# A hybrid diffusion layer: the inverse of the second recurrence multiplied head by head, outputs stored in two pieces a half step, operands loaded by halves of the heads

## The chip, the core and the metric

The kernel runs on one core of a Trainium2 chip. The metric is the device time of one execution in microseconds (us), lower is better. A core has five engines with queues of their own: TensorE (PE) multiplies matrices into PSUM, VectorE (DVE), ScalarE (ACT) and GpSimd (POOL) work element by element, and SyncE (SP) issues the transfers between memory (HBM) and the on-chip SBUF, which 16 DMA engines carry out. Each engine works through its instructions in the order in which the program has them, and waits where one needs a result that isn't there.

## The reference

One layer on 1024 latent tokens and 256 context tokens, 1024 channels wide, all in fp32. A normalised and modulated input goes through one projection into two token mixers: a gated linear recurrence (RG-LRU) and RWKV-7. Their outputs are gated, projected, merged and added to the input; a SwiGLU channel mixer and a last normalisation follow. The change lies in RWKV-7's recurrence, which has 16 heads of 64 channels and runs over the tokens in both directions (`d` = 2), with the context's final state as the start of the latent scan:

```python
def step(S, inp):
    r_t, w_t, k_t, v_t, a_t, b_t = inp
    sa = jnp.einsum('dbhij,dbhj->dbhi', S, a_t)
    S = S * w_t[..., None, :] + sa[..., :, None] * b_t[..., None, :] + v_t[..., :, None] * k_t[..., None, :]
    y = jnp.einsum('dbhij,dbhj->dbhi', S, r_t)
    return S, y
```

The outputs of both directions are added, normalised per head (group norm), joined by a bonus term and multiplied by a gate.

## The kernel before

The program has stages. `phase_ux` and `phase_a2` compute the projections and prepare RWKV-7's operands; `phase_b` runs its recurrence, with the output projection of the RG-LRU as fill; `phase_c1` and `phase_c2` do the merge, the output projection and the channel mixer.

The recurrence works in chunks of 32 tokens: 40 steps, of which steps 0 to 7 are the context and 8 to 39 the latent tokens. Each step handles one chunk in either direction for 16 heads, 32 units of a direction and a head. They are cut into two halves of 8 heads (`a` = 0, 1), and `wkv_chain(k, a)` is a generator that issues one half's work. Inside a chunk the serial dependence is solved by the inverse of a 32 by 32 triangular matrix per unit, made in `phase_a2` by VectorE (`wkv_inverse`, tile `X`), written to HBM as `x_d` and loaded for four steps at a time as `xc`.

One half step is this chain:

- `ru`, first part (line 1034): 16 products of 128 rows by 32 columns, `skb` with `tvu`, into PSUM; a copy brings them to SBUF as `rs` (line 1036).
- `ru`, second part (lines 1045 and 1046): the inverse times `rs`. The four units that stand at partitions 0, 32, 64 and 96 are done by one product of 128 by 128 whose left side is block-diagonal. That left side is the tile `xbd`, cleared once; four VectorE copies a step put the blocks of `xc` into it (line 1025), for both halves, in two tiles that take turns.
- Four copies of 32 partitions bring the result into `tvu` (line 1048), on VectorE and ScalarE in turn (`copy`, line 993).
- `pn` (line 1054): 16 products of 128 rows by 64 columns, the next state; two copies or scalings bring it into the next step's `tvu` (lines 1059 and 1063).
- `py` (line 1005), for latent steps: 16 products, a copy to `ys`, and four stores to `y_d` of 32 rows by 256 numbers (line 1013).

`tvu` has two buffers a half; its rows of v are loaded one step ahead (`new_tvu`, line 969). `wkv_load` (line 982) loads a step's `skb` (1 MB) and `ska` (0.5 MB) into a ring of three, 8 KB a partition in one piece, once both halves are done with the step two before.

In `phase_b` the two halves are drawn in a fixed pattern (line 1158), and between them products of the fill (`pol`, line 1107) in a number that grows with the step. The first eight steps are given a priority over the end of `phase_a2`, which prepares the last heads' operands (`pm`, `pkt`, `pz`) and the last inverses. From step 28 on the group norms of finished token blocks run beside the chain (`norms`, `group_norm`), each loading y of both directions whole (line 1246). A scheduler orders the instructions of each engine by priorities and its own estimate of times, so the order on an engine isn't the order in the code. PSUM tiles that two engines read are read in turn.

Of the kernel before, what the change touches and what calls it, by code (L numbers as in the profile page):

```python
# [16 lines left out]
P = 128  # L17
D = 1024
KD = D // P
SEQ = 1024  # L20
# [887 lines left out]
FILLA = 0  # L908
ROUNDS = ((0, 1), (2, 3), (4, 5), (6, 7), (8,), (9,))
FPTS = ((0, 0), (38, 1), (40, 1))  # L910
UT = 0
NEND = 3
SETV = 0
SETDVE = 0
XDVE = 40
XACT = 0
PACE = 1
MORE = (1, 2, 3)
NRD = 3
# [6 lines left out]
NRING = 3  # L926
# [3 lines left out]
def wkv_setup(k):  # L930
    nc, bp = k.nc, k.bp
    z = lambda n, sh: bp.tile(sh, F32, name=n)
    k.ska = [z(f"ska{i}", [P, NU, 64]) for i in range(NRING)]
    k.skb = [z(f"skb{i}", [P, NU, 64]) for i in range(NRING)]
    for i, t in enumerate(k.ska):
        nc.scalar.copy(t[0:64], bcast(k.ident[0:64, 0:64], 1, NU))
    if not UT:
        k.xbd = [z(f"xbd{i}", [P, 8, 4, 32]) for i in range(2)]
        for t in k.xbd:
            (nc.vector if SETDVE & 2 else nc.gpsimd).memset(t, 0.0)  # L940
    k.tvu = [[z(f"tvu{a}_{i}", [P, 2, 8, 64]) for i in range(2)] for a in range(2)]
    k.pb = z("pb", [P, 2, 20, KD])
    for i, e in ((1, slice(16, 20)), (0, slice(0, 16))):
        for d in range(2):
            nc.sync.dma_start(k.pb[64 * d:64 * d + 64, :, e].rearrange("p h e j -> p h (e j)"),
                              k.pd_d[i][:, d].rearrange("(h p) f -> p h f", p=64))
    k.xc = {}
# [17 lines left out]
def new_tvu(k, s, a):  # L965
    nc = k.nc
    src = pair(k.v_d.rearrange("(c s) f -> c s f", s=32), chunk_id(s, 0), chunk_id(s, 1))
    t = k.tvu[a][s % 2]
    nc.sync.dma_start(t[64:96].rearrange("p d h i -> p d (h i)"), src[:, :, a * 512:a * 512 + 512].rearrange("d s f -> s d f"))
    return t  # L970


def wkv_load(k, s):
    nc = k.nc
    ska, skb = k.ska[s % NRING], k.skb[s % NRING]
    if s % 4 == 0:
        xc = k.bpool.tile([P, 4, 2, 4, 32], F32, name=f"xc{s}", tag="xc", bufs=2)
        nc.sync.dma_start(xc.rearrange("p n a v t -> p (n a v t)"), (k.x_d[:, s - 8:s - 4] if s >= 8 else k.xc_d[:, s:s + 4]).rearrange("p s f -> p (s f)"))
        k.xc[s // 4] = xc
    lat, c = s >= 8, s - 8 if s >= 8 else s  # L980
    for t, src in ((skb, k.skb_d), (ska[64:P], k.ska_d)):
        nc.sync.dma_start(t.rearrange("p u f -> p (u f)"), src[not lat][c].rearrange("r u f -> r (u f)"))


def wkv_chain(k, a):

    nc, pool, ps = k.nc, k.bpool, k.psb

    def mm(*a, **b):
        k.pe_last = nc.tensor.matmul(*a, **b, start=True, stop=True).ins.name  # L990

    def copy(out, src):
        (nc.vector.tensor_copy if k.turn % 5 in COPYD else nc.scalar.copy)(out, src)  # L993
        k.turn += 1

    unit = lambda d, i: d * NH + a * 8 + i
    units = [(v, g, slice(32 * g, 32 * g + 32), g // 2, (g % 2) * 4 + v) for v in range(4) for g in range(4)]

    def outputs(s, tvu):
        if s < 8:  # L1000
            return
        skb = k.skb[s % NRING]
        py = k.psb2.tile([P, 4, 64], F32, name=f"py{s}_{a}", tag="py", bufs=1)
        for v, g, gr, d, i in units:
            mm(py[gr, v], skb[:, unit(d, i), 0:32], tvu[:, d, i])
        ys = k.op.tile([P, 256], F32, name=f"ys{s}_{a}", tag="ys", bufs=4)
        copy(ys, py.rearrange("p v i -> p (v i)"))
        for d in range(2):
            r = 32 * chunk_id(s, d)
            for h in range(2):  # L1010
                g = 2 * d + h
                c = a * 512 + h * 256
                nc.sync.dma_start(k.y_d[d, r:r + 32, c:c + 256], ys[32 * g:32 * g + 32])

    cur, nxt, prev = None, new_tvu(k, 0, a), None
    for t in k.tvu[a]:
        (nc.vector if a < SETV else nc.gpsimd).memset(t[96:P], 0.0)
    for s in range(NSTEP):
        ska, skb = k.ska[s % NRING], k.skb[s % NRING]
        if not UT:  # L1020
            xb = k.xbd[s % 2]
        if a == 0 and not UT:
            for g in range(4):
                gr = slice(32 * g, 32 * g + 32)
                (nc.scalar.copy if s < XACT else nc.vector.tensor_copy if s < XDVE else nc.gpsimd.tensor_copy)(xb[gr, :, g], k.xc[s // 4][gr, s % 4].rearrange("p a v t -> p (a v) t"))
        prev, tvu = cur, nxt
        cur = tvu
        ahead = lambda: new_tvu(k, s + 1, a) if s + 1 < NSTEP else None
        if a == 1:
            nxt = ahead()  # L1030
        t = ps.tile([P, 2, 4, 64], F32, name=f"ru{s}_{a}", tag="ru", bufs=2)
        seen = slice(0 if s else 64, P)
        for v, g, gr, d, i in units:
            mm(t[gr, 0, v], skb[seen, unit(d, i), 32:64], tvu[seen, d, i])
        r = pool.tile([P, 4, 64], F32, name=f"rs{s}_{a}", tag="rs", bufs=2)
        copy(r, t[:, 0])
        yield
        if a == 0:
            if s > 0:
                outputs(s - 1, prev)  # L1040
            nxt = ahead()
            yield
        for v, g, gr, d, i in units if UT else ():
            mm(t[gr, 1, v], k.xc[s // 4][gr, s % 4, a, v], r[gr, v])
        for v in range(0 if UT else 4):
            mm(t[:, 1, v], xb[:, a * 4 + v].rearrange("p a b -> p (a b)"), r[:, v])
        for g in range(4):
            copy(tvu[96:P, g // 2, g % 2 * 4:g % 2 * 4 + 4], t[32 * g:32 * g + 32, 1])
        yield
        if nxt is not None:  # L1050
            pn = (k.psb2 if a and s >= 8 else ps).tile([P, 8, 64], F32, name=f"pn{s}_{a}", tag="pn", bufs=1)
            for i in range(8):
                for d in range(2):
                    mm(pn[64 * d:64 * d + 64, i], ska[0 if s else 64:P, unit(d, i)], tvu[0 if s else 64:P, d, i])
            for d in range(2):
                h = slice(64 * d, 64 * d + 64)
                nt = nxt[0:64, d]
                if s % 2 == 0:
                    copy(nt, pn[h])
                else:  # L1060
                    b1, c1 = chunk(s + 1, d)
                    pv = k.pb[h, :, b1 * 2 + c1 // 2, a * 4:a * 4 + 4].rearrange("p h j -> p j h")
                    nc.vector.tensor_tensor(nt.rearrange("p (j h) i -> p j h i", h=2), pn[h].rearrange("p (j h) i -> p j h i", h=2), bcast(pv, 3, 64), ALU.mult)
        yield
        if a == 1:
            outputs(s, tvu)
            yield
    if a == 0:
        outputs(NSTEP - 1, cur)
        yield  # L1070
# [67 lines left out]
def phase_b(k):  # L1138
    tc = k.tc
    k.gnp = k.root.enter_context(tc.tile_pool(name="gnp", bufs=1, side="right"))  # L1140
    with tc.tile_pool(name="bp", bufs=1) as k.bp, tc.tile_pool(name="olp", bufs=1) as op, \
# [9 lines left out]
        with tc.high_priority(offset=SETO):  # L1151
            wkv_setup(k)
            for s in range(NRING):
                wkv_load(k, s)
        k.turn = 0
        halves = [wkv_chain(k, a) for a in range(2)]
        for s in range(NSTEP + 1):
            for i, a in enumerate((0, 0, 1, 0, 1, 1, 0, 1)):
                if s == 0 and i in (2, 4) or s == NSTEP and i not in (1, 2, 4):
                    continue  # L1160
                if s < CTXP:
                    prio_next(k, halves[a], CTXO)
                else:
                    next(halves[a])
                if i == 4 and s - 1 + NRING < NSTEP:
                    wkv_load(k, s - 1 + NRING)
                if i == 4:
                    k.step = s - 1
                if i == 4 and s == 28:
                    back = norms(k, k.gnp, pso)  # L1170
                if (s, i) >= (28, 4):
                    next(back, None)
                k.pe_after = k.pe_last
                if i in FILLAT:
                    at = s + (FILLAT.index(i) + 1) / len(FILLAT)
                    while done < (480 - FILL0 - TAIL) * (at + CTXW * min(at, 8)) / (NFEND + 8 * CTXW):
                        next(fill, None)
                        done += 1
                k.pe_after = None
# [54 lines left out]
def group_norm(k, pool, ps, tb, out=None):  # L1234
# [7 lines left out]
    flat = lambda t: t.rearrange("p a i -> p (a i)")  # L1242
    y, v, g = big("gy"), big("gv"), big("gg")
    y1 = k.c1p.tile([P, NH, 64], F32, name="gy1_7") if tb == 7 else big("gy1")
    for t, src in ((v, k.v_d), (g, k.gate_d), (y, k.y_d[0]), (y1, k.y_d[1])):
        nc.sync.dma_start(flat(t), src[tok])
        for _ in range(GNY):
            yield
    yield
# [251 lines left out]
def scratch(k):  # L1501
# [13 lines left out]
    k.x_d = t("x_d", [P, NSTEP - 8, 256])  # L1515
    k.pd_d = [t(f"pd{i}_d", [P, 2, n * KD]) for i, n in enumerate((16, 4))]
    k.t1_d = t("t1_d", [D, SEQ])
    k.y_d = t("y_d", [2, SEQ, D])


@with_exitstack
# [174 lines left out]
```

## Time and profile before

| | us |
|---|---|
| median of 3 runs (3169.22 to 3175.68) | 3172.0 |
| the profiled execution | 3170.86 |
| its span | 3168.8 |
| TensorE busy (87%) | 2772.7 |
| VectorE busy (63%) | 2010.8 |
| ScalarE busy (45%) | 1410.4 |
| GpSimd busy (33%) | 1037.3 |

The recurrence begins near 1500 us and ends near 2195. Beside its first 200 us the stage before it ends; in its last 200 us the group norms run. From about 2230 us to the end the span is the merge and the channel mixer, with TensorE nearly without a gap. TensorE's granted clock is a share of 2.4 GHz and has two levels, 1 and 0.5; a mean between them tells how long it was at either. Busy time of TensorE includes the modelled ends of its products, so a stretch in which small products follow each other with pauses of a few hundred ns still counts as busy.

### The profile page before, as it was taken

What the parts mean: (1) busy time and instruction counts of PE and PEld (TensorE: products, weight loads), DVE (VectorE), ACT (ScalarE), POOL (GpSimd) and SP (SyncE); (2) the same over time, 40 slices, a digit from 0 to 9 for tenths busy, and PEclk for the clock granted to TensorE, in tenths of its full rate; (3) what the DMA queues carried; (4) which work ended last, traced back from release to release, by engine and by line L of the source; (5) the groups of instructions that cost most, each with busy time, mean ns of one, the idle gap of its engine ahead of it and who ended that gap; (6) DMA issues with size and microseconds to landing.
All of it is one profiled execution on the core that took longest, in us unless ns stands there. A gap on an engine that the chain in (4) does not pass through costs nothing. (4 is left out here: it accounts for less than half of the span.)

```text
span 3168.8 us, 53672 instructions
## 1 busy us (share of the span) xinstructions
PE 2772.7 (87%) x20606; PEld 2235.2 (71%) x20606; DVE 2010.8 (63%) x3067; ACT 1410.4 (45%) x2579; POOL 1037.3 (33%) x896
## 2 busy tenths in 40 slices
PE   5888888789898878887889878788899999999998
PEld 4767666667777666765666767566678888888888
DVE  7688989894667887878874434675686423232234
ACT  3465757474467555767333433344425111111114
POOL 4344435452445545666333220323441000000000
PEclk9999899999899878987558978788999999999999
DMA  5334333322455455555766777776772211111112
GB/s 201 105 107 128 115 109 118 111 76 74 142 145 143 114 123 128 131 140 136 192 189 213 220 210 206 222 240 220 266 284 85 98 57 54 37 57 40 46 57 71
DMA packets 374726, 428.96 MB, mean 135 GB/s; under 512 B 135446, under 2 KB 279238, under 8 KB 366534
## 3 DMA queue, kind: packets, MB, share of 16 engines
q1 hardware_dynamic: 374470, 425.53, 45.4%
q8 instruction: 163, 2.67, 0.4%
q14 instruction: 93, 0.76, 0.1%
HBM read 286.87 MB, written 126.26 MB: 130 GB/s over the span
## 5 line engine op out<-in xcount | busy, mean ns | idle before, releaser
L88 PE MATMUL pin<-h1024hi,whi 128*128 128x512 f32 (+1 forms) x1024 | 431.9, 422 | 47.0 <-DVE whi L230 15.2
L90 PE MATMUL pin<-h1024hi,wlo 128*128 128x512 f32 (+1 forms) x1024 | 425.8, 420 | 26.0 <-POOL wlo L231 16.8
L89 PE MATMUL pin<-h1024lo,whi 128*128 128x512 f32 (+1 forms) x1024 | 427.2, 417 | 4.1 <-DVE h1024lo L120 4.1
L231 POOL TENSOR_TENSOR wlo<-wraw,whi 128x512 fp32r<-128x512 f32 (+1 forms) x144 | 229.7, 1595 | 339.8 <-DVE whi L230 135.0
L88 PEld LDWEIGHTS pin<-h1024hi,whi 128*128 128x128 f32 (+1 forms) x1024 | 205.2, 201 | 100.8 <-DVE whi L230 21.3
L90 PEld LDWEIGHTS pin<-h1024hi,wlo 128*128 128x128 f32 (+1 forms) x1024 | 204.8, 200 | 80.6 <-POOL wlo L231 23.1
L89 PEld LDWEIGHTS pin<-h1024lo,whi 128*128 128x128 f32 (+1 forms) x1024 | 204.2, 199 | 51.3 <-DVE h1024lo L120 6.6
L54 ACT ACT_TABLE_LOAD x164 | 210.4, 1283 | 17.2 <-DVE gd L499 5.9
L990 PE MATMUL pn<-tvu,ska 128*64 128x64 f32 (+1 forms) x2496 | 159.8, 255 | 34.9 <-DVE tvu L993 20.1
L1444 DVE TENSOR_TENSOR sil<-sil,pfu 128x512 f32<-128x512 f32 x44 | 30.2, 687 | 243.2 <-PE pfu L90 243.2
L990 PEld LDWEIGHTS pn<-tvu,ska 128*64 128x64 f32 (+1 forms) x2496 | 122.8, 161 | 75.9 <-DVE tvu L993 23.3
L388 DVE SCALAR_TENSOR_TENSOR lxc<-lup,c_lru_conv_w,lxc 120x512 f32<-120x512 f32 (+3 forms) x198 | 159.4, 835 | 0.4
L1452 DVE SCALAR_TENSOR_TENSOR x<-pfo,modv,x 128x512 f32<-128x512 f32 (+1 forms) x112 | 74.2, 670 | 132.4 <-PE pfo L90 132.4
L990 PE MATMUL ru<-tvu,skb 128*32 128x64 f32 (+1 forms) x2560 | 107.7, 260 | 49.9 <-ACT tvu L993 26.0
L993 ACT COPY tvu<-ru 32x256 f32<-32x256 f32 x193 | 69.9, 362 | 151.8 <-DVE tvu L993 99.4
L68 ACT CAST whi_fi<-wraw_fi 128x1024 fp32r<-128x1024 f32 x48 | 50.6, 1053 | 168.3 <-PE pfg L89 53.0
L990 PE MATMUL ru<-rs,xbd 128*128 128x64 f32 x640 | 113.3, 335 | 12.4 <-ACT rs L993 8.3
L415 PE MATMUL pg<-lh,gw 120*120 120x512 f32 (+3 forms) x264 | 95.4, 373 | 32.4 <-DVE lh L398 29.7
L990 PEld LDWEIGHTS ru<-tvu,skb 128*32 128x32 f32 (+1 forms) x2560 | 69.5, 131 | 75.9 <-ACT tvu L993 28.5
L680 ACT COPY bc<-pm 32x256 f32<-32x256 f32 x160 | 98.5, 616 | 52.6 <-PE pm L676 50.3
L721 DVE TENSOR_TENSOR X<-X,it 128x62 f32<-128x62 f32 (+25 forms) x186 | 119.1, 640 | 3.9
L720 DVE TENSOR_TENSOR it<-bp,X 128x62 f32<-128x62 f32 (+25 forms) x186 | 118.3, 636 | 3.8
(374 smaller groups left out, 7660.8 us busy)
## 6 DMA issues: line engine op xcount, KB each, us to landing
skb<-skb_d SPq DMA_DIRECT2D x40, 1024.0 KB
wraw<-in_w_in_dram SPq DMA_DIRECT2D x142, 256.0 KB
wraw_fi<-in_w_ffn_in_dram SPq DMA_DIRECT2D x48, 512.0 KB
skb_d<-kr SPq DMA_DIRECT2D x160, 128.0 KB
ska_d<-km SPq DMA_DIRECT2D x160, 128.0 KB
skb_d<-km SPq DMA_DIRECT2D x160, 128.0 KB
ska<-ska_d SPq DMA_DIRECT2D x40, 512.0 KB
wmr<-in_w_modT_dram SPq DMA_DIRECT2D x32, 512.0 KB
```

The source lines that it names most:

```text
L54: ins = self.nc.scalar.activation(*a, **b).ins
L88: nc.tensor.matmul(out, wh, xh, start=first, stop=False)
L89: nc.tensor.matmul(out, wh, xl, start=False, stop=False)
L90: nc.tensor.matmul(out, wl, xh, start=False, stop=last)
L231: (nc.gpsimd if INLO else nc.vector).tensor_tensor(lo, raw, hi.bitcast(F32), ALU.subtract)
L388: nc.vector.scalar_tensor_tensor(xc, tap(j), k.lcw[r, t, d, j:j + 1], xc, ALU.mult, ALU.add)
L415: nc.tensor.matmul(pg[r, g, 0:w], gw[r, v, g * LT:g * LT + rows(t)], m, start=(x == 0), stop=(x == len(passes) - 1))
L680: nc.scalar.copy(bc[g, :, 4 * i:4 * i + 4].rearrange("s t e h -> s h e t"), pm[64 * c + 32:64 * c + 64, :, d, :, 32:64])
L720: nc.vector.tensor_tensor(tv, bpt[:, :, t + 1:32, t:t + 1].to_broadcast(sh), X[:, :, t:t + 1, 0:t + 1].to_broadcast(sh), ALU.mult)
L721: nc.vector.tensor_tensor(X[:, :, t + 1:32, 0:t + 1], X[:, :, t + 1:32, 0:t + 1], tv, ALU.add)
L990: k.pe_last = nc.tensor.matmul(*a, **b, start=True, stop=True).ins.name
L1452: nc.vector.scalar_tensor_tensor(x, p[:, 0:n], k.modv[:, 40 + o, 0:1], x, ALU.mult, ALU.add)
```

## The change

There are four parts. The inverse's products are issued unit by unit: 16 of 32 by 32 a half step, whose left sides are read from `xc` directly; `xbd`, its clearing and its copies go. `tvu` has three buffers and v is loaded two steps ahead. `y_d` is laid out by direction, chunk, quarter of the channels and token, so that a half step stores 64 partitions at once, two stores instead of four; the group norm reads it back by chunks, four loads a direction instead of one. `wkv_load` loads one half's heads, in two pieces of 2 KB a partition, half 0 right after its own outputs and half 1 after its own.

```diff
-    if not UT:
-        k.xbd = [z(f"xbd{i}", [P, 8, 4, 32]) for i in range(2)]
-        for t in k.xbd:
-            (nc.vector if SETDVE & 2 else nc.gpsimd).memset(t, 0.0)
-    k.tvu = [[z(f"tvu{a}_{i}", [P, 2, 8, 64]) for i in range(2)] for a in range(2)]
+    k.tvu = [[z(f"tvu{a}_{i}", [P, 2, 8, 64]) for i in range(3)] for a in range(2)]
...
-def wkv_load(k, s):
+def wkv_load(k, s, a):
...
-    if s % 4 == 0:
+    if s % 4 == 0 and a == 0:
...
-        nc.sync.dma_start(t.rearrange("p u f -> p (u f)"), src[not lat][c].rearrange("r u f -> r (u f)"))
+        h = lambda x: x.rearrange("p (d a i) f -> p d a (i f)", d=2, a=2)[:, :, a]
+        nc.sync.dma_start(h(t), h(src[not lat][c]))
...
         for d in range(2):
-            r = 32 * chunk_id(s, d)
-            for h in range(2):
-                g = 2 * d + h
-                c = a * 512 + h * 256
-                nc.sync.dma_start(k.y_d[d, r:r + 32, c:c + 256], ys[32 * g:32 * g + 32])
+            nc.sync.dma_start(k.y_d[d, chunk_id(s, d), 2 * a:2 * a + 2].rearrange("h t f -> (h t) f"), ys[64 * d:64 * d + 64])
...
-        if a == 0 and not UT:
-            for g in range(4):
-                gr = slice(32 * g, 32 * g + 32)
-                (nc.scalar.copy if s < XACT else nc.vector.tensor_copy if s < XDVE else nc.gpsimd.tensor_copy)(xb[gr, :, g], k.xc[s // 4][gr, s % 4].rearrange("p a v t -> p (a v) t"))
...
-        cur = tvu
-        ahead = lambda: new_tvu(k, s + 1, a) if s + 1 < NSTEP else None
+        cur, nxt = tvu, nn
+        ahead = lambda: new_tvu(k, s + 2, a) if s + 2 < NSTEP else None
...
-        for v, g, gr, d, i in units if UT else ():
+        for v, g, gr, d, i in units:
             mm(t[gr, 1, v], k.xc[s // 4][gr, s % 4, a, v], r[gr, v])
-        for v in range(0 if UT else 4):
-            mm(t[:, 1, v], xb[:, a * 4 + v].rearrange("p a b -> p (a b)"), r[:, v])
...
-                if i == 4 and s - 1 + NRING < NSTEP:
-                    wkv_load(k, s - 1 + NRING)
+                if i in (1, 4) and 0 < s and s - 1 + NRING < NSTEP:
+                    wkv_load(k, s - 1 + NRING, i // 4)
...
-    for t, src in ((v, k.v_d), (g, k.gate_d), (y, k.y_d[0]), (y1, k.y_d[1])):
-        nc.sync.dma_start(flat(t), src[tok])
+    for t, src in ((v, k.v_d), (g, k.gate_d), (y, 0), (y1, 1)):
+        if t is v or t is g:
+            nc.sync.dma_start(flat(t), src[tok])
+        else:
+            for c in range(4):
+                nc.sync.dma_start(flat(t)[32 * c:32 * c + 32].rearrange("t (b f) -> t b f", f=256),
+                                  k.y_d[src, 4 * tb + c].rearrange("b t f -> t b f"))
...
-    k.y_d = t("y_d", [2, SEQ, D])
+    k.y_d = t("y_d", [2, SEQ // 32, 4, 32, 256])
```

The scheduler places the new instructions, and with them others. TensorE in step 1, where half 0's `pn` and half 1's inverse products meet. Names carry the step and the half: `pn1_0` is `pn` of step 1, half 0. Before:

```order
L990 MATMUL pn1_0_15168<-tvu0_1_14854,ska1_14841 64x64
L612 MATMUL pz7_768_0_14433<-lora0_0_6258,lwl7_14126 128x256
L612 MATMUL pz7_768_0_14433<-lora1_0_6372,lwh7_14125 128x256
L612 MATMUL pz7_768_0_14433<-lora1_0_6372,lwl7_14126 128x256
L990 MATMUL ru1_1_15149<-rs1_1_15166,xbd1_14850 128x64 x4
L667 MATMUL pkt7_256_1_14332<-c_ident_84,kb7_256_1_14322 128x128 x4
L692 MATMUL pbn7_256_14387<-c_rkblk_6145,kd07_256_0_14295 128x2 x2
L990 MATMUL pn1_0_15168<-tvu0_1_14854,ska1_14841 64x64 x15
```

And at the same place now:

```order
L984 MATMUL pn1_0_15206<-tvu0_1_14850,ska1_14841 64x64
L612 MATMUL pz7_768_0_14433<-lora1_0_6372,lwh7_14125 128x256
L612 MATMUL pz7_768_0_14433<-lora1_0_6372,lwl7_14126 128x256
L984 MATMUL pn1_0_15206<-tvu0_1_14850,ska1_14841 64x64 x6
L984 MATMUL ru1_1_15187<-rs1_1_15204,xc0_14860 32x64 x7
L984 MATMUL pn1_0_15206<-tvu0_1_14850,ska1_14841 64x64
L984 MATMUL ru1_1_15187<-rs1_1_15204,xc0_14860 32x64
```

The four large inverse products stood in one piece, and `pn` behind them; the sixteen small ones begin inside `pn`, and the last two rows repeat eight times more, one product of either kind at a time.

VectorE in steps 14 and 15: the copies of `ru`, `pn` and `py` belong to the chain, `xbd0` is the left side for step 16. Before:

```order
L993 COPY tvu0_1_14854<-pn14_0_17012 64x512
L993 COPY ys14_0_17084<-py14_0_17067 128x256
L993 COPY tvu1_0_14855<-ru14_1_16993 32x256
L1025 COPY xbd0_14849<-xc16_16988 32x8x32 x4
L993 COPY tvu1_0_14855<-ru14_1_16993 32x256
L993 COPY tvu0_1_14854<-ru15_0_17048 32x256
```

And now:

```order
L987 COPY tvu0_0_14849<-pn14_0_17312 64x512
L987 COPY tvu1_2_14854<-ru14_1_17293 32x256 x2
L987 COPY ys14_0_17392<-py14_0_17375 128x256
L987 COPY tvu0_0_14849<-ru15_0_17356 32x256
L1094 TENSOR_TENSOR olg0_6_16829<-pol0_6_16832,olg0_6_16829 128x512
L987 COPY tvu0_0_14849<-ru15_0_17356 32x256
```

The four copies between half 1's two `tvu` copies are gone, and its two copies follow each other.

SP in steps 13 and 14, all of it transfers (`ska`, `skb` the operands, `tvu` the rows of v, `y_d` the stores). Before:

```order
L982 DMA ska1_14841<-ska0_d_70 64x2048
L982 DMA skb1_14844<-skb0_d_68 128x2048
L1013 DMA y_d_77<-ys13_1_16982 32x256 x4
L969 DMA tvu1_1_14856<-v_d_67 32x2x512
L969 DMA tvu0_0_14853<-v_d_67 32x2x512
L1013 DMA y_d_77<-ys14_0_17084 32x256 x4
```

And now:

```order
L976 DMA skb1_14844<-skb0_d_68 128x2x512
L1003 DMA y_d_77<-ys13_0_17217 64x256 x2
L976 DMA ska1_14841<-ska0_d_70 64x2x512
L976 DMA skb1_14844<-skb0_d_68 128x2x512
L1003 DMA y_d_77<-ys13_1_17286 64x256 x2
L961 DMA tvu1_1_14853<-v_d_67 32x2x512
L976 DMA ska2_14842<-ska0_d_70 64x2x512
```

A store of either half now has half the instructions, and the operands' loads stand in more and smaller pieces between them.

## Rows read from the trace of the kernel before

**Rows 1.** Windows: length; busy us (count) of PE, PEld, DVE, ACT, POOL; clock; DMA.

```profile
1500.00:1700.00 200.00, 166.30 (x1547) 125.33 (x1546) 153.45 (x272) 71.65 (x149) 67.78 (x67) 0.57 0.70 192
1700.00:1998.00 298.00, 256.26 (x4674) 208.92 (x4672) 119.54 (x260) 103.43 (x230) 64.78 (x44) 0.87 0.73 215
1998.00:2196.00 198.00, 152.22 (x2377) 118.92 (x2372) 132.80 (x179) 88.56 (x227) 65.48 (x29) 0.77 0.71 217
...
2376.00:3168.00 792.00, 783.32 (x3595) 654.75 (x3593) 285.66 (x407) 188.15 (x304) 15.72 (x6) 1.00 0.19 60
```

**Rows 2.** The chain of waits, its earliest piece: start us, us, what.

```profile
2209.81 2.39 ACT gy L1263 x10
```

**Rows 3.** Timeline of TensorE, high clock, then low: start us, us, engine, line, operation, count.

```profile
1906.52 1.10 PE L990 MATMUL ru<-rs,xbd 128*128 128x64 f32 x8
...
1908.43 0.63 PE L990 MATMUL ru<-tvu,skb 128*32 128x64 f32 x32
...
1690.72 1.97 PE L990 MATMUL ru<-rs,xbd 128*128 128x64 f32 x8
1692.62 1.07 PE L990 MATMUL ru<-tvu,skb 128*32 128x64 f32 x28
```

**Rows 4.** Timeline of TensorE, the fill's products at the high clock, then the low.

```profile
1911.59 0.40 PE L1107 MATMUL pol<-llo,olh 128*128 128x512 f32 x1
1911.83 0.39 PE L1107 MATMUL pol<-lhi,oll 128*128 128x512 f32 x1
...
1694.21 0.63 PE L1107 MATMUL pol<-lhi,oll 128*128 128x512 f32 x1
1694.64 0.63 PE L1107 MATMUL pol<-llo,olh 128*128 128x512 f32 x1
```

**Rows 5.** Timeline of TensorE where two shapes alternate, low clock, then high.

```profile
1681.24 0.42 PE L990 MATMUL ru<-tvu,skb 128*32 128x64 f32 x2
1681.59 0.48 PE L990 MATMUL pn<-tvu,ska 128*64 128x64 f32 x2
1682.00 0.42 PE L990 MATMUL ru<-tvu,skb 128*32 128x64 f32 x2
...
1916.27 0.31 PE L990 MATMUL ru<-tvu,skb 128*32 128x64 f32 x4
1916.51 0.33 PE L990 MATMUL pn<-tvu,ska 128*64 128x64 f32 x2
```

**Rows 6.** Timeline of VectorE around the copies of two steps.

```profile
1808.02 1.24 DVE L1025 COPY xbd<-xc 32x256 f32<-32x256 f32 x4
1809.29 0.88 DVE L993 COPY tvu<-ru 32x256 f32<-32x256 f32 x2
...
2051.99 5.24 DVE L1025 COPY xbd<-xc 32x256 f32<-32x256 f32 x4
```

**Rows 7.** Groups by line, VectorE, 1700 to 2196: count, busy us, mean ns, idle before.

```profile
L1025 DVE COPY xbd<-xc 32x256 f32<-32x256 f32 x124 | 53.5, 432 | 31.1 <-PE ru L990 28.2
```

**Rows 8.** Waits of TensorE, 1700 to 2196: us in total, times, longest us.

```profile
PE ru L990 <- ACT tvu L993: 21.8, 10, 8.0
PE pn L990 <- DVE tvu L993: 10.5, 4, 3.3
PE pn L990 <- ACT tvu L993: 10.0, 7, 3.4
```

**Rows 9.** Timeline of SP: the last inverse's store and its load for step 8.

```profile
1676.52 0.92 SPq L740 DMA_DIRECT2D x_d<-xo  x2
...
1689.36 0.37 SPq L978 DMA_DIRECT2D xc<-x_d  x1
```

**Rows 10.** Timeline of SP: the four stores of one half step.

```profile
1822.50 1.93 SPq L1013 DMA_DIRECT2D y_d<-ys  x4
```

**Rows 11.** The chain of waits: two transfers that it waited for.

```profile
2264.54 5.25 DMA wmr<-in_w_modT_dram
...
2271.10 3.29 DMA gr<-gr_d
```

More of the change, by code (lines that the diff above doesn't have):

```diff
@@ L910 @@
 FPTS = ((0, 0), (38, 1), (40, 1))
-UT = 0
 NEND = 3
 SETV = 0
-SETDVE = 0
-XDVE = 40
-XACT = 0
 PACE = 1
@@ L967, in new_tvu @@
     src = pair(k.v_d.rearrange("(c s) f -> c s f", s=32), chunk_id(s, 0), chunk_id(s, 1))
-    t = k.tvu[a][s % 2]
+    t = k.tvu[a][s % 3]
     nc.sync.dma_start(t[64:96].rearrange("p d h i -> p d (h i)"), src[:, :, a * 512:a * 512 + 512].rearrange("d s f -> s d f"))
     return t
-def wkv_load(k, s):
+def wkv_load(k, s, a):
     nc = k.nc
     ska, skb = k.ska[s % NRING], k.skb[s % NRING]
-    if s % 4 == 0:
+    if s % 4 == 0 and a == 0:
         xc = k.bpool.tile([P, 4, 2, 4, 32], F32, name=f"xc{s}", tag="xc", bufs=2)
@@ L1008, in outputs @@
         for d in range(2):
-            r = 32 * chunk_id(s, d)
-            for h in range(2):
-                g = 2 * d + h
-                c = a * 512 + h * 256
-                nc.sync.dma_start(k.y_d[d, r:r + 32, c:c + 256], ys[32 * g:32 * g + 32])
-    cur, nxt, prev = None, new_tvu(k, 0, a), None
+            nc.sync.dma_start(k.y_d[d, chunk_id(s, d), 2 * a:2 * a + 2].rearrange("h t f -> (h t) f"), ys[64 * d:64 * d + 64])
+    cur, nxt, nn, prev = None, new_tvu(k, 0, a), new_tvu(k, 1, a), None
     for t in k.tvu[a]:
@@ L1019, in wkv_chain @@
         ska, skb = k.ska[s % NRING], k.skb[s % NRING]
-        if not UT:
-            xb = k.xbd[s % 2]
-        if a == 0 and not UT:
-            for g in range(4):
-                gr = slice(32 * g, 32 * g + 32)
-                (nc.scalar.copy if s < XACT else nc.vector.tensor_copy if s < XDVE else nc.gpsimd.tensor_copy)(xb[gr, :, g], k.xc[s // 4][gr, s % 4].rearrange("p a v t -> p (a v) t"))
         prev, tvu = cur, nxt
-        cur = tvu
-        ahead = lambda: new_tvu(k, s + 1, a) if s + 1 < NSTEP else None
+        cur, nxt = tvu, nn
+        ahead = lambda: new_tvu(k, s + 2, a) if s + 2 < NSTEP else None
         if a == 1:
-            nxt = ahead()
+            nn = ahead()
         t = ps.tile([P, 2, 4, 64], F32, name=f"ru{s}_{a}", tag="ru", bufs=2)
@@ L1040, in wkv_chain @@
                 outputs(s - 1, prev)
-            nxt = ahead()
+            nn = ahead()
             yield
-        for v, g, gr, d, i in units if UT else ():
+        for v, g, gr, d, i in units:
             mm(t[gr, 1, v], k.xc[s // 4][gr, s % 4, a, v], r[gr, v])
-        for v in range(0 if UT else 4):
-            mm(t[:, 1, v], xb[:, a * 4 + v].rearrange("p a b -> p (a b)"), r[:, v])
         for g in range(4):
@@ L1153, in phase_b @@
             for s in range(NRING):
-                wkv_load(k, s)
+                for a in range(2):
+                    wkv_load(k, s, a)
         k.turn = 0
```

## The prediction

> **What bounds the kernel now.** I read the windows first, because the change touches one stage only. Four stretches matter [rows 1]: 1500 to 1700 us (steps 0 to 7 of the second recurrence, beside the last work of the stage before it), 1700 to 1998 (steps 8 to 27), 1998 to 2196 (steps 28 to 39, with the group norms beside them) and 2376 to the end. In the last one TensorE is busy 783.32 of 792 us at a granted clock of 1.00, so a microsecond gained before it moves that block forward and is kept. The chain of waits can be followed back to the normalisation of the last token blocks [rows 2], which needs the last step's stores: the recurrence is on the path.
>
> Inside the recurrence no engine is full. TensorE is busy 166.30 of 200, 256.26 of 298 and 152.22 of 198 us, at a granted clock of 0.57, 0.87 and 0.77 [rows 1]. With levels of 1.2 and 2.4 GHz (0.5 and 1) that is 14%, 74% and 54% of the time at the high one. So TensorE holds the pace five sixths of the time, and the chain product, copy, product through VectorE and ScalarE the rest.
>
> **The change part by part, against the profiled execution: 3170.86 us for a span of 3168.8, 1.1 us under the median of 3172.0.**
>
> *The inverse's products.* Before, a half step has 4 products of 128 rows by 128 columns, 8 instructions (fp32 takes two each): 1.10 us at the high clock, 1.97 at the low one. Now it has 16 products of 32 by 32, 32 instructions. No row shows this shape. The nearest is the 128-row by 32-column product, four of which share the array: 32 instructions in 0.63 us, and 28 in 1.07 at the low clock, so 1.22 for 32 [rows 3]. Taking that, a half step saves 0.47 or 0.75 us: 16 half steps before step 8 at (0.14, 0.86) give 11 us, 40 in steps 8 to 27 at (0.74, 0.26) give 22, 24 after that at (0.54, 0.46) give 14. Upper end: 32 rows against 128 could overlap further; even at nothing for the new products the saving is 1.10 a half step. Lower end: they don't overlap at all, which is a rival below.
>
> *Changes of shape.* The array takes one tile shape at a time. Where `pn` (64 columns) and `ru` (32 columns) alternate by two instructions, a change comes every 0.35 to 0.41 us at the low clock, and 0.24 at the high one [rows 5]; less the products themselves (two at 0.03 to 0.05) a change costs about 0.30 and 0.19. In the order of TensorE's instructions I counted the changes: before step 8 there are 224 and now 344, in steps 8 to 27 215 and now 263, after that 156 and now 168. The 120 new ones before step 8 come from the scheduler: sixteen small products are laid one by one between the other half's sixteen `pn`, where four large ones stood in one piece. Price: 120 by 0.28 is 34 us, 48 by 0.22 is 10, 12 by 0.24 is 3.
>
> *Fill that moves.* By the same count 46 of the `pol` products leave steps 0 to 7 and 51 more stand in steps 8 to 27, 5 fewer after. They follow each other by 0.23 us at the high clock and 0.43 at the low one [rows 4]. In an in-order queue they cost only where TensorE has no gap, so I weight them with its busy share: 46 by 0.40 by 0.83 is 15 us off the first stretch, 51 by 0.28 by 0.86 is 12 onto the second, 1 off the third.
>
> So TensorE's account is 34 - 11 - 15 = +8, -22 + 10 + 12 = 0, and -14 + 3 - 1 = -12. However short the first stretch gets, step 8 must wait for its data: the last of the inverse is stored at 1676.5 and its load for step 8 issued at 1689.4 [rows 9].
>
> *The VectorE copies.* All 160 copies into `xbd` go. From 1700 to 2196 they are 124 with 53.5 us busy, 432 ns mean [rows 7]; four take 1.24 us, and 5.24 at the worst [rows 6]. They stand between two copies of the chain: at 1808.02 the four run, and the next `tvu` copy begins 0.03 us after them [rows 6]. Since the products that follow (`pn`) need all four of a half's `tvu` copies, this delays one half in each step. The bounds are 0 (the other half's products fill TensorE meanwhile) and 53.5. TensorE has 88 us of idle time in these two stretches, and waits for the chain's copies are what fills them (21.8 and 10.5 us are the two largest) [rows 8]. One half of two is delayed, and not always with TensorE idle: I take two fifths, 22 us. Late next is the `tvu` copy itself, behind its neighbour on ScalarE. Before step 8 the copies are hidden by the first stretch's own TensorE work, at nothing.
>
> *Stores and loads.* Each store took 0.48 us to issue on SP [rows 10]. A half step issues 2 where it issued 4, a step's operands take 4 where they took 2, and a group norm's y takes 8 where it took 2: 128 fewer, 80 and 48 more, nothing in sum. Only the last norm's 6 extra issues stand on the path: +3 us. The operands' 2 KB pieces instead of 8 KB: the nearest rows are 256 KB in 2 KB pieces in 3.29 us and 512 KB in 4 KB pieces in 5.25 [rows 11], 78 and 98 KB a microsecond with the fixed part in both. At best there is no difference; at worst the 1.5 MB of a step take a quarter longer, with the DMA engines at a 0.73 share [rows 1], and part of that would be late. One half's load is now issued earlier in the step, and v two steps ahead instead of one, so I take nothing, and keep +15 for the range. The three buffers of `tvu` take the room that `xbd` leaves.
>
> Sum: +8 + 0 - 12 - 22 + 3 = -23 us, so 3148 by the profiled execution and 3149 against the median.
>
> The sixteen new products of a half step write one tile, `ru`, whose 2 KB a partition are one PSUM bank, from four row groups. The Trainium skill (TensorEngine Tiling (Array Packing), Restrictions and Gotchas) says that different row tiles cannot access one PSUM bank at the same time; no run here shows two row tiles in one bank, and by that rule the sum would be the fourth rival's, by the rows above it is the forecast's.
>
> **The rivals.** *1. The changes of shape decide (slower).* Place: steps 0 to 7. If a change costs the full 0.38 us of the row and the fill that left had only filled gaps, this stretch gains 120 by 0.38 less 11, +34 us; if in addition the other half hides the copies, only the -12 and +3 remain: +25, or 3196. It decides once the first eight steps end 20 us later than before. For it: the low clock there and the alternation in the order. Against it: 34 us of idle TensorE time in this stretch, and the fill that left.
>
> *2. TensorE holds the pace throughout (no change).* The copies on VectorE were hidden, their 22 us fall away: -1, or 3170. For it: 86% busy in steps 8 to 27, where TensorE's account is 0. Against it: the copies' place in the middle of the chain.
>
> *3. The stalls on loads go too (much faster).* The 21.8 us of `ru` behind ScalarE's `tvu`, with 10.0 of `pn`, come from a ScalarE that itself stands behind the fill's loads. With smaller operand loads in the queue, and half the stores, these could land in time: -23 - 32, or 3117. For it: single waits up to 8.0 us [rows 8]. Against it: as many issues on SP as before, and as many bytes.
>
> *4. The small products don't overlap.* Four instructions on different columns take 4 by 0.013 us in the 0.63 us row, so one alone 0.052 and 32 of them 1.9 us, 3.7 at the low clock: 0.8 or 1.7 us more than before in a half step. That is 25 + 41 + 29 us on TensorE, in place of 47 saved: -23 + 47 + 95 = +119, or 3290. Rows of `ru` speak against it, but those have four column tiles and one row tile. The page's rule on banks, above, is this case.
>
> **How the numbers follow.** The forecast has 0.50, with its own range of 3128 to 3165 (two fifths of 53.5 may be none or all, less the loads' +15). Rival 1 has 0.15, rival 2 0.17, rival 3 0.14, rival 4 0.04. A measurement of this kernel can tell about 0.2% from no change, 6 us. Faster by more than that: 0.46 of the forecast, 0.14 of rival 3, 0.06 of rival 2, together 0.66. Within it: 0.10 of rival 2, 0.02 of the forecast and 0.01 of rival 1, 0.13. Slower: 0.13 and 0.04 of rivals 1 and 4, and 0.04 of the rest, 0.21. The range that leaves out two in ten reaches to rival 1 on one side and past rival 3 on the other: 3106 to 3196.
>
> **What would show it.** In the new profile 32 instructions of `ru` from `xc` should take near 0.63 us at the high clock; 1.9 shows rival 4. No VectorE row between two `tvu` copies of one half should come from the inverse. Step 8's first products should come within 10 us of where they did; 20 us later is rival 1. The stretch of steps 8 to 39 should shrink by 30 to 40 us with TensorE's busy share up; if the share rises with the length unchanged, it is rival 2. ScalarE's waits for loads should be as long as before; if they halve, rival 3. The forecast is wrong if the recurrence ends no earlier than 2185.

## The result, and the profile after

The changed kernel takes 3148.6 us (median of 6 runs, 3142.3 to 3159.7) against 3173.7 for the kernel before in the same session: a ratio of 0.9927, with a 95% interval of 0.9905 to 0.9949, or 25 us by the medians. The forecast was 3149. The number was right; several of the terms behind it were not, and the experiments below show which.

Windows of the changed kernel, columns as in [rows 1]:

```profile
1500.00:1700.00 200.00, 177.24 (x1828) 122.64 (x1831) 133.41 (x237) 66.30 (x143) 56.96 (x61) 0.55 0.68 177
1700.00:1998.00 298.00, 248.55 (x5867) 189.11 (x5860) 92.84 (x175) 111.25 (x241) 75.14 (x52) 0.91 0.83 235
1998.00:2196.00 198.00, 145.31 (x2895) 109.45 (x2889) 110.78 (x149) 93.04 (x239) 74.80 (x32) 0.81 0.83 233
...
2376.00:3146.00 770.00, 760.85 (x3495) 635.92 (x3493) 265.84 (x376) 174.85 (x281) 8.64 (x3) 1.00 0.19 60
```

Against [rows 1], TensorE is busier in the first stretch (177 for 166 us) and less busy in the next two (249 for 256, 145 for 152); VectorE loses 20 to 27 us in each; the DMA share rises from 0.73 and 0.71 to 0.83. The last block is what it was, only earlier: the chain of waits has the same step of it in both kernels, before and then after.

```profile
2357.19 1.73 PE ss_f L1405 x8
```
```profile
2195.71 2.15 ACT gy L1251 x9
...
2334.74 1.73 PE ss_f L1393 x8
```

It starts 22.45 us earlier, and the span is 22.4 us shorter (3146.4 for 3168.8): all of the gain is made before it. The step of [rows 2] comes at 2195.71, 14.1 us earlier; the other 8 appear in the transition behind it.

The products `py` give the outputs of steps 8 to 39, so their first and last start mark that stretch (count, ns, first to last start). Before, and then after:

```profile
L990 PE MATMUL py<-tvu,skb x2048: 216/219/317, 1708.7 to 2193.7; 128*32 128x64 f32 x187
```
```profile
L984 PE MATMUL py<-tvu,skb x2048: 216/219/317, 1716.1 to 2180.3; 128*32 128x64 f32 x187
```

Step 8's output comes 7 us later, the stretch takes 464.2 us for 485.0, and from its end to the step at 2357.19 (now 2334.74) it is 154.4 us for 163.5. So of the 22 us, 13 are won by the end of the recurrence and 9 behind it.

TensorE's timeline, high clock, then low, then a piece of steps 0 to 7 where the shapes alternate (start us, us, engine, line, operation):

```profile
1894.83 0.65 PE L984 MATMUL ru<-rs,xc 32*32 32x64 f32 x32
1895.41 0.50 PE L1089 MATMUL pol<-llo,olh 128*128 128x512 f32 x1
...
2006.96 1.08 PE L984 MATMUL ru<-rs,xc 32*32 32x64 f32 x32
...
1549.01 0.42 PE L984 MATMUL ru<-rs,xc 32*32 32x64 f32 x2
1549.36 0.47 PE L984 MATMUL pn<-tvu,ska 128*64 128x64 f32 x2
1549.76 0.42 PE L984 MATMUL ru<-rs,xc 32*32 32x64 f32 x2
```

The 32 small products of a half step take 0.65 us at the high clock and 1.08 at the low one, where the eight large ones took 1.10 and 1.97 [rows 3]. I had taken 0.63 and 1.22 from another shape. All 32 write one tile of 2 KB a partition, and each product reads 32 partitions and writes the 32 of the same number: four row groups, each with one column group of its own.

TensorE's waits between 1700 and 2196 us (us in total, times, longest):

```profile
PE pn L984 <- ACT tvu L987: 17.4, 10, 3.6
...
PE pn L984 <- DVE tvu L987: 4.9, 6, 1.6
...
PE ru L984 <- ACT tvu L987: 3.7, 3, 3.1
```

Of the three waits in [rows 8], 42.3 us together, 26.0 are left; the one on ScalarE's `tvu` in front of `ru` fell from 21.8 to 3.7.

### The profile page after: what moved, and what is told of

Same layout as the page of the kernel before. It is cut to its first block, busy times and chain, and to the rows that moved or that the text cites. A ratio compares the mean times of both kernels' runs of the same rounds, so it can differ in the third digit from the quotient of the medians.

```text
span 3146.4 us, 57347 instructions
## 1 busy us (share of the span) xinstructions
PE 2754.8 (88%) x22526; PEld 2192.1 (70%) x22526; DVE 1936.4 (62%) x2907; ACT 1412.0 (45%) x2579; POOL 1030.2 (33%) x896
## 5 line engine op out<-in xcount | busy, mean ns | idle before, releaser
L984 PE MATMUL pn<-tvu,ska 128*64 128x64 f32 (+1 forms) x2496 | 172.5, 260 | 31.3 <-ACT tvu L987 17.7
L984 PEld LDWEIGHTS pn<-tvu,ska 128*64 128x64 f32 (+1 forms) x2496 | 130.8, 165 | 71.1 <-issue 27.7
L987 DVE COPY tvu<-ru 32x256 f32<-32x256 f32 x127 | 53.7, 423 | 118.8 <-ACT tvu L987 92.8
L230 DVE CAST whi<-wraw 128x512 fp32r<-128x512 f32 (+1 forms) x144 | 76.3, 530 | 65.2 <-PE pin L89 29.7
L984 PE MATMUL ru<-rs,xc 32*32 32x64 f32 x2560 | 89.9, 247 | 29.4 <-ACT rs L987 13.1
```

Of the source, the lines that this page charges most:

```text
L230: nc.vector.tensor_copy(hi, raw)
```

## The experiments

Each was timed with the kernel before on the same chip, and all ratios are to it. 0.001 is 3.2 us. Short names: I is the inverse unit by unit, S the new layout of `y_d` with two stores, L the operands by halves, T the third `tvu` buffer. The change is I+S+L+T.

| run | median us | ratio | 95% interval |
|---|---|---|---|
| e1: I | 3139.97 | 0.9906 | 0.9882 to 0.9930 |
| e2: S | 3155.06 | 0.9948 | 0.9927 to 0.9968 |
| e3: L | 3176.21 | 1.0019 | 1.0006 to 1.0033 |
| e4: I+S+L | 3156.04 | 0.9948 | 0.9927 to 0.9969 |
| e5: I+S | 3114.20 | 0.9839 | 0.9818 to 0.9861 |
| e6: I+S+T | 3135.47 | 0.9904 | 0.9883 to 0.9925 |
| e7: I+L | 3154.77 | 0.9959 | 0.9939 to 0.9979 |
| e8: change + idle copies | 3158.77 | 0.9969 | 0.9954 to 0.9985 |
| e9: change, TensorE by groups | 3137.14 | 0.9888 | 0.9870 to 0.9905 |
| e10: I+S + 8 KB taken | 3130.34 | 0.9874 | 0.9854 to 0.9894 |
| e11: I + two stores by tokens | 3182.18 | 1.0044 | 1.0027 to 1.0062 |
| e12: I+S, L from step 11 | 3138.52 | 0.9896 | 0.9880 to 0.9911 |

**e1, the inverse alone.**

```diff
-UT = 0
+UT = 1
```

> The kernel before with the inverse's products unit by unit and nothing else of the change (no xbd, no copies into it; loads, stores and two tvu buffers as before). Theory 1 (the gain is the inverse's: copies gone from VectorE's chain, shorter products): 3145 to 3156 us, the whole gain of the changed kernel within 6 us. Theory 2 (the gain is the loads and stores: ScalarE's and TensorE's stalls behind transfers, 21.8 us of ru behind ScalarE's tvu before and 3.7 after): 3168 to 3176, no change. In both, a half step's 32 small products take 0.58 us at the high clock and 1.01 at the low one.

30 us faster, more than the whole change: theory 2 falls as an account of the gain, and theory 1 is short, since something else in the change costs time. The 32 small products took 0.65 and 1.08 us here too, not 0.58 and 1.01. The recurrence also starts earlier than before: see e10. `py` in e1:

```profile
L990 PE MATMUL py<-tvu,skb x2048: 216/219/317, 1691.5 to 2175.2; 128*32 128x64 f32 x187
```

In this execution, 22 us shorter than before, step 8's output comes 17 us earlier, and steps 8 to 39 take 483.7 us for 485.0. The forecast had the inverse win 34 us net in that stretch; this trace doesn't show them there.

**e2, the stores alone; e3, the loads alone.** Both edits are those of the change.

> The kernel before with the new layout of y_d alone (two stores a half step, a group norm's y in four pieces for each direction). Theory 1: 3171 to 3177 (three more microseconds for the last norm's loads at most). Theory 2: 3160 to 3168, since 128 fewer stores stand in the queue before the operands' loads.

> The kernel before with a step's operands loaded by halves of the heads in 2 KB pieces, one half issued earlier in the step, and nothing else. Theory 1: 3169 to 3177, no change. Theory 2: 3155 to 3165, since the stalls behind loads go.

I had priced both at nothing. S gains 16 us by its ratio, more than theory 2 had it; L loses 6, still within theory 1. SP shows where S gains. Its longest waits between 1700 and 2130 us (us in total, times, longest), the kernel before:

```profile
SPq L1013 <- DMA skb<-skb_d: 52.5, 18, 4.1
...
SPq L1013 <- DMA ska<-ska_d: 13.7, 11, 2.1
```

and e2, where line 1009 is the store:

```profile
SPq L1009 <- DMA skb<-skb_d: 13.7, 6, 2.6
```

Before, SP waited 66 us in front of stores for what the profile takes to be the operands' own transfers; with half as many stores, 14 for `skb`, and `ska` is below the list's smallest (8.1). Other waits grew in exchange: SP's wait for `pn` before an operand's load from 21.5 to 37.1 us, and that of the group norms' loads for the stores from 7.6 to 28.5. What stands behind them on SP is the next `v` and the fill's loads. A piece of SP's timeline before, four stores and what follows:

```profile
1803.46 1.91 SPq L1013 DMA_DIRECT2D y_d<-ys  x4
1805.42 2.02 SPq L969 DMA_DIRECT2D tvu<-v_d  x2
1807.91 4.73 SPq L1013 DMA_DIRECT2D y_d<-ys  x4
```

and in e2:

```profile
1807.87 1.23 SPq L1009 DMA_DIRECT2D y_d<-ys  x2
1809.15 1.35 SPq L969 DMA_DIRECT2D tvu<-v_d  x2
1810.63 1.09 SPq L1009 DMA_DIRECT2D y_d<-ys  x2
```

With the waits between them, the four stores of a half step took 2.5 us of SP's time in the median between 1700 and 2130 us and up to 5.6; the two in e2 took 1.15 and up to 3.1. So the price of a store was more than the 0.48 us of [rows 10], in the queue that feeds every engine. `py` in e2:

```profile
L990 PE MATMUL py<-tvu,skb x2048: 219/219/316, 1720.0 to 2167.1; 128*32 128x64 f32 x187
```

Steps 8 to 39 take 447.1 us for 485.0, 38 less. The span is only 13 us shorter: step 8 comes 11 us later, though nothing was edited ahead of it, and the rest is lost behind the recurrence. Whether S gains by the number of its stores alone, or also by the 64 KB of a store that now lie in one piece of memory, isn't shown; e11 was to tell them apart and brought in something else.

**e4, e5 and e7, two and three of the parts.**

> The changed kernel with two tvu buffers instead of three, v loaded one step ahead as before; inverse, stores and loads as changed. Theory 1: 3145 to 3153, as the changed kernel, since the third buffer was priced at nothing. Theory 2: 3155 to 3165, since v two steps ahead is part of what makes the loads land in time.

> The kernel before with the inverse unit by unit and the new layout of y_d; operands loaded whole, two tvu buffers. Theory 1 (the two gains are in different resources, VectorE's and TensorE's chain and SP's issuing, and the loads by halves took them back): 3122 to 3134 us, about the sum of the 29 and 14 us that they gained alone. Theory 2 (both gains are one and the same slack): 3137 to 3146, no better than the inverse alone. In both, the last of the first stage's inversion on VectorE ends at 1672 to 1683 us, as in the kernels with whole loads.

> The kernel before with the inverse unit by unit and the operands loaded by halves; stores and tvu buffers as before. Theory 1 (loads by halves delay the inversion on VectorE in the first eight steps, which then sets when step 8 starts): its last operation ends at 1688 to 1700 us instead of 1674, and the time is 3150 to 3165. Theory 2 (halves cost only their issues on SP, the 7 us that they cost alone): 3143 to 3150, with the inversion ending near 1675.

I+S gains 51 us, a little more than the sum of the two (30 + 16) and than theory 1 of e5 had it: the two add up. `py` in e5, and TensorE's wait for the rows of v between 1700 and 2196 us, in e1 and then in e5:

```profile
L990 PE MATMUL py<-tvu,skb x2048: 216/219/316, 1686.9 to 2133.1; 128*32 128x64 f32 x187
```
```profile
PE ru L990 <- DMA tvu<-v_d: 21.9, 8, 8.9
```
```profile
PE ru L990 <- DMA tvu<-v_d: 1.0, 2, 0.6
```

With the inverse alone, `ru` waited 22 us for rows of v, whose loads stand behind the stores on SP; with two stores that wait is gone, and steps 8 to 39 take 446.2 us for e1's 483.7.

With L added the gain is 16 (e4), so on top of I+S the loads by halves cost 35 us, on top of I 17 (e7), by themselves 6. These are kernels with two `tvu` buffers; with three, L costs 7 (the change against e6, 0.9927 for 0.9904, intervals that overlap). e4 and the change (0.9948 and 0.9927) have intervals that overlap too; the third buffer's worth beside the halves stays open. In e7 the last inversion on VectorE ends later, as theory 1 had it. The transposes right behind the four inversions (count, ns, first and last start) show it. Before:

```profile
L729 DVE STREAM_TRANSPOSE xo<-X x4: 1900/1924/2019, 1520.5 to 1671.9; 64x1024 f32<-64x1024 f32 x4
```

The changed kernel:

```profile
L729 DVE STREAM_TRANSPOSE xo<-X x4: 1907/1952/1989, 1515.1 to 1694.0; 64x1024 f32<-64x1024 f32 x4
```

I+S (e5), then I+L (e7):

```profile
L729 DVE STREAM_TRANSPOSE xo<-X x4: 1902/1949/1958, 1509.2 to 1671.3; 64x1024 f32<-64x1024 f32 x4
```
```profile
L729 DVE STREAM_TRANSPOSE xo<-X x4: 1897/1906/1928, 1511.4 to 1689.0; 64x1024 f32<-64x1024 f32 x4
```

Step 8's inverse can't start before this last one is stored and loaded again [rows 9]. In the change it comes 22 us later than before. One trace tells this within some 10 us: in the four kernels that are alike up to step 7 (e1, e5, e11, e12) the last transposes start at 1665.6 to 1675.1, and in e2 at 1680.9. Step 8 itself is less late than the inversion. Before, the load of its inverse was issued at 1689.4 and its first copy came only at 1706.2, so step 8 waited for the chain; in the change the load is issued at 1703.0 and that copy comes at 1704.3, both together. In e5 the chain is there first (step 8's first `ru` product at 1645.0, the load issued at 1678.4) and does wait for the inversion.

**e12, the halves from step 11 on.**

```diff
+HALF = 11
-                if i == 4 and s - 1 + NRING < NSTEP:
-                    wkv_load(k, s - 1 + NRING)
+                n = s - 1 + NRING
+                if i == 4 and n < min(NSTEP, HALF):
+                    wkv_load(k, n)
+                if i in (1, 4) and HALF <= n < NSTEP:
+                    wkv_load(k, n, i // 4)
```

> The kernel with the inverse unit by unit, the new layout of y_d and two tvu buffers, operands whole up to step 10 and by halves from step 11 on, so that the first stage sees whole loads. Theory 1 (halves cost in the first eight steps, where the inversion on VectorE ended 10 to 20 us later with them): 3110 to 3121, as with whole loads. Theory 2 (halves cost SP's issues in the later steps, 41 us in all there): 3130 to 3150.

18 us slower than e5 (0.9896 for 0.9839): theory 2. The last inversion is early here, and steps 8 to 39 are long:

```profile
L729 DVE STREAM_TRANSPOSE xo<-X x4: 1897/1930/1962, 1502.9 to 1665.8; 64x1024 f32<-64x1024 f32 x4
```
```profile
L995 PE MATMUL py<-tvu,skb x2048: 217/219/318, 1682.0 to 2165.2; 128*32 128x64 f32 x187
```

So these 18 us are lost in the later steps (483.2 us for 446.2 in e5), and by subtraction the other 17 of the 35 between e4 and e5 in the first ones. In the later steps three things differ together: 2 issues more on SP, 2 KB pieces (four of them took 4 x 119 ns, counted over all of that size, where one of 8 KB took 445 in e5), and the place in the order. These weren't tried apart.

**e9, TensorE's order by groups.**

```diff
+        if k.grp and k.pe_last:
+            k.tc.add_manual_dep(ins, k.pe_last, NOSYNC, reason="group")
+        k.grp = False
...
+        k.grp = s < 8
```

The last line stands ahead of each of the three groups of a half step.

> The changed kernel with TensorE's order in steps 0 to 7 held by groups: the first product of each group of the recurrence is set behind the last of the group before it in the program (an order without a wait), so that the sixteen small products of the inverse stand in one piece again; some 220 changes of shape fewer. Theory 1 (the forecast's price, 120 changes at 0.28 us or 34 us in these steps, delays the first stage's inversion on VectorE, which starts step 8): the inversion ends 10 to 25 us before the changed kernel's 1693.8 us, and the time is 3125 to 3140. Theory 2 (the changes stand where TensorE would have waited): the inversion ends as before, 3143 to 3153.

12 us faster than the change (0.9888 for 0.9927, intervals that only touch), and the inversion ends 26 us earlier: theory 1, at a smaller price. Windows, last transposes and `py` of e9:

```profile
1500.00:1600.00 100.00, 65.23 (x1343) 53.11 (x1343) 77.12 (x150) 38.09 (x86) 26.73 (x37) 0.65 0.86 217
1600.00:1700.00 100.00, 55.16 (x954) 38.92 (x953) 57.64 (x99) 34.38 (x66) 41.66 (x29) 0.69 0.68 201
```
```profile
L729 DVE STREAM_TRANSPOSE xo<-X x4: 1906/1916/1934, 1510.1 to 1668.1; 64x1024 f32<-64x1024 f32 x4
```
```profile
L984 PE MATMUL py<-tvu,skb x2048: 216/219/316, 1687.4 to 2161.0; 128*32 128x64 f32 x187
```

TensorE is busy 120 of 200 us there, 177 in the change. I counted the changes of shape in the traces, from the recurrence's first product to the last inversion: 190 before, 328 in the change, 253 in e1, e5 and e12, 318 in e4 and e7, 260 in e3, 109 in e9. So with two buffers I adds 63, and L 65 to 70: with the loads in halves the scheduler lays the two halves' products one between the other. Where the third buffer or its room is taken there are as many without L (298 in e6, 295 in e10), and L adds 30. 219 changes fewer moved the inversion by 26 us, 0.12 us each if all of it is theirs; e9 also starts 5 us earlier, and its edit orders whatever stands between the groups. Step 8's output comes 29 us earlier than in the change, but only 12 are left at the end: in these two traces steps 8 to 39 take 9 us more (473.6 for 464.2), and the rest goes behind the recurrence. That L's delay in e3, e4 and e7 is these changes fits the counts and isn't shown; e9 shows it for TensorE's order in the change itself.

**e6 and e10, the third buffer and its room.** e6 is the change with whole loads; e10 takes 8 KB a partition in the pool and does nothing with them.

```diff
+    k.junk = [z(f"junk{i}", [P, 2, 8, 64]) for i in range(2)]
+    for t in k.junk:
+        nc.gpsimd.memset(t[96:P], 0.0)
```

> The changed kernel with the operands loaded whole (inverse, stores and the three tvu buffers as changed). Theory 1 (the third buffer is worth nothing by itself): within 5 us of the run with two buffers. Theory 2 (v two steps ahead is worth the 7 us by which the changed kernel is ahead of its version with two buffers): 5 to 10 us less than the run with two buffers.

> The kernel with the inverse unit by unit, the new layout of y_d, whole loads and two tvu buffers, with 8 KB a partition taken in its pool by a tile that nothing reads (memset once, as a third buffer is), so that only the room of the third buffer is put back. Theory 1 (the room decides when the second recurrence may start, since it lies where the stage before still works): its first copy on ScalarE comes at 1483 to 1489 us instead of 1473, and the time is 3126 to 3138, near the 3135 of the kernel with three buffers. Theory 2 (the earlier loads of v cost it): 3111 to 3119.

Neither theory of e6 held: without L the buffer costs 20 us. e10 explains about half of it: the room alone costs 11 (0.9874 for 0.9839, intervals that overlap by 0.0007). ScalarE's first copies of the recurrence, before, in e5 and in e10:

```profile
L936 ACT COPY ska<-c_ident x3: 1893/1895/1898, 1487.0 to 1490.6; 64x2048 f32<-64x2048 f32 x3
```
```profile
L936 ACT COPY ska<-c_ident x3: 1896/1897/1897, 1473.5 to 1477.1; 64x2048 f32<-64x2048 f32 x3
```
```profile
L936 ACT COPY ska<-c_ident x3: 1895/1896/1899, 1485.7 to 1489.3; 64x2048 f32<-64x2048 f32 x3
```

Without the 8 KB the recurrence starts 13 us earlier; with them it starts where it did. The room also changes TensorE's order (295 changes of shape for 253 in e5), so its 11 us are not the start alone. The kernel before held them as `xbd`, the change holds them as the third buffer. The other 9 us, by which e6 is behind e10, are within what the two intervals leave open; the earlier loads of `v` are the candidate.

**e8, the copies alone.**

```diff
+        if a == 0:
+            for g in range(4):
+                gr = slice(32 * g, 32 * g + 32)
+                nc.vector.tensor_copy(k.junk[gr], k.xc[s // 4][gr, s % 4].rearrange("p a v t -> p (a v) t"))
```

> The changed kernel with the four copies a step from xc on VectorE put back, into a tile that nobody reads: their price by itself, without the large products. Theory 1 (the copies stand in the chain): 12 to 25 us above the changed kernel, 3160 to 3173. Theory 2 (they are hidden, and the inverse gains by its shorter products on TensorE): 3146 to 3153, as the changed kernel.

10 us above the change by the medians, 13 by the ratios (0.9969 for 0.9927, intervals apart): the copies stand in the chain, at the lower end of theory 1. They also changed TensorE's order (292 changes of shape, last inversion 1677), which may hide some of their price, and their tile takes 1 KB a partition of the pool, which wasn't tried apart.

**e11, two stores by tokens.** One transfer of [2, 32, 256] rows in place of two of [32, 256].

```diff
-            for h in range(2):
-                g = 2 * d + h
-                c = a * 512 + h * 256
-                nc.sync.dma_start(k.y_d[d, r:r + 32, c:c + 256], ys[32 * g:32 * g + 32])
+            nc.sync.dma_start(k.y_d[d, r:r + 32, a * 512:a * 512 + 512].rearrange("t (h f) -> h t f", h=2), ys[64 * d:64 * d + 64])
```

> The kernel with the inverse unit by unit, whole loads and two tvu buffers, and y_d by tokens as before, but stored by one transfer for both half-blocks (two a half step, rows of 1 KB at a stride), so that a group norm reads y in two transfers and not eight. Theory 1 (the gain of the stores is their number on SP, and the six extra issues of a norm are lost time): 3102 to 3113 us, at or below the 3114 of the kernel with the new layout. Theory 2 (the gain is the 64 KB in one piece of memory): 3125 to 3140, near the inverse alone.

Neither: 43 us slower than e1, with as few stores as e5. The stores' own issue is short, but SP is held at some of the loads behind them (count, ns least, median and most, between 1720 and 2110 us). e1 and e11:

```profile
L969 SPq DMA_DIRECT2D tvu<-v_d x53: 315/392/1458, 1722.3 to 2108.4; - x53
```
```profile
L969 SPq DMA_DIRECT2D tvu<-v_d x48: 308/424/4660, 1750.5 to 2099.2; - x48
```

and the DMA share of 1700 to 2130 us falls to 0.70 (e1 0.77, e5 0.81). The Trainium skill (DMA: Bandwidth & Descriptors, Why a DMA increments its semaphore by 16 and not by 1) says that a transfer is spread over the largest number of engines, up to 16, that divides the slowest dimension of both its patterns. By that rule this store, whose slowest dimension is 2, runs on two engines, and those of e1 and e5, with 32 and 64, on all sixteen. The traces don't name the engines, but their packets agree with it: between 1700 and 2130 us packets of 1 KB, which are the stores', were under way for 210 us in e11, one or two at a time for 199 of them, and for 93 us in e1, up to 18 at a time.

## Why the prediction was right, point by point

**What bounds the kernel.** Held: the recurrence was on the path, and what was won before the last block reached the end whole (22.45 us). That step 8 waits for the inversion was named, but not that this could move.

**The sum by stretches.** The forecast had +8 us before step 8's outputs, -34 in steps 8 to 39 (0, -12 and -22) and +3 behind them; by the rows of `py` it was +7, -21 and -9. The middle was a third short, and 9 us behind the recurrence, which the forecast didn't have and no run explains, made up for it. That the sum hit the number is luck. The sign given for steps 8 to 39, 30 to 40 us shorter with TensorE's busy share up, didn't come: the share fell from 86 to 83% and from 77 to 73%.

**The inverse's products.** Their duration held: 0.65 and 1.08 us measured for 0.63 and 1.22. Rival 4 is out: the 32 instructions into one tile took 0.65 us, not 1.9. The Trainium skill (TensorEngine Tiling (Array Packing), Restrictions and Gotchas) says that different row tiles cannot access one PSUM bank at the same time. In the time of these 0.65 us nothing of it is seen, but each row group here has a column group of its own; no run shows two row groups that share one.

**Changes of shape.** Right that they come and where; the term was mis-sized. 34 us were priced for steps 0 to 7 and balanced by 26 of shorter products and fill, so step 8 was to come 8 us later. Step 8's first copy came within 2 us of before (1704.3 for 1706.2 us) and its output 7 us later, as forecast, while the inversion came 22 us later and now arrives together with the chain. The price of TensorE's order by e9 is 12 us of the time, with 219 changes fewer; 0.12 us each at the inversion, where 0.28 were taken.

**The copies.** Right in kind: 22 taken, 13 measured (e8, beside the rest of the change).

**The inverse as a whole.** The terms +8, 0, -12 and -22 give -26; e1 measured -30. But part of that is the room: `xbd` went, and e1 starts the recurrence early. The prediction said that the third buffer takes this room and gave it no price; e10 gives 11 us, which leaves about -19 for the inverse itself.

**Stores and loads.** This step failed: "128 fewer, 80 and 48 more, nothing in sum". An issue is not worth its own 0.48 us but what it holds up. S gained 16 alone and 21 beside I. L lost 6 alone, 35 beside I and S, beyond the bound of +15, and 7 where the third buffer is there too; that buffer, priced at nothing, cost 20 without L. The sum of the terms came out because what was missed has both signs: the stores, against the loads, the buffer and its room.

**The rivals.** 1 had the right place, as the busier TensorE of the first stretch and the inversion's end show, but its sign, step 8 20 us later, didn't come. 2 is out for the change, by e8: the copies weren't hidden. 3 had a true sign in it: the wait of `ru` on ScalarE fell from 21.8 to 3.7 us. It falls with I alone (12.2), S alone (15.3) and L alone (14.6), and to 5.0 with I and S; so the smaller loads aren't its cause by themselves, and alone they cost 6 us. ScalarE's own waits for the fill's loads didn't halve: for the three largest it is 57.5 us before and 60.5 after.

The version with the inverse and the stores alone (e5), 3114.2 us and 0.9839 of before, beats both kernels. Grouping TensorE's products in the first eight steps, which helped the change, wasn't tried on it.

## What to carry to other kernels

A forecast that sums to the right number is no proof of its terms: run each part alone, and then in pairs, since the loads by halves cost 6 us alone, 35 beside two other parts and 7 beside all three. Check the sum stretch by stretch, too: here one stretch made up for another. Price a DMA issue by what stands behind it in its queue, and a buffer by whom its room keeps waiting in the stage before. Where an edit makes instructions smaller, count how the scheduler interleaves them, above all ahead of a chain that sets a later start.

## What the runs showed that I had not expected

Four row groups, each with a column group of its own and all writing one tile of 2 KB a partition, took 0.65 us for 32 fp32 instructions at the high clock, as fast as four column groups over all rows (0.63) [rows 3]. Eight KB a partition that nobody reads cost about 11 us (e10, intervals that just overlap). And merging two stores into one with a leading dimension of 2 made the kernel 43 us slower than the four separate ones (e11).
